# A hybrid encoder step: 28 pairs of input projections computed as seven block products, ahead of the attention

## The chip, the core and the metric

One core of one Trainium2 chip. The metric is the device time of one execution of the whole step in microseconds (us); lower is better. The engines are named as in the profile: PE multiplies matrices and writes PSUM, PEld is its loading of weights, DVE is the vector engine, ACT the engine of the activation functions, POOL the GpSimd engine, SP the queue from which nearly all DMAs are issued. Each engine takes its instructions in program order.

## The reference

A thousand and twenty-four new frames (the prompt) and 32 frames of a running stream (the sample) go through one layer. Both are 1024 channels wide, and the kernel treats them as 1056 columns. All inputs are float32.

```python
def mixer_inputs(x, norm_g, w_in, b_f, q_g, k_g):
    h = rmsnorm(x, norm_g)
    cols = lambda a, w: h @ w_in[:, a:a + w]
    q = rmsnorm(cols(OFF_Q, ATTN_WIDTH).reshape(B, T, N_HEADS, HEAD_DIM), q_g) * (HEAD_DIM ** -0.5)
    k = rmsnorm(cols(OFF_K, ATTN_WIDTH).reshape(B, T, N_HEADS, HEAD_DIM), k_g)
    v = cols(OFF_V, ATTN_WIDTH).reshape(B, T, N_HEADS, HEAD_DIM)
    logf = jax.nn.log_sigmoid((cols(OFF_F, N_HEADS) + b_f).astype(jnp.float32))
    ga = cols(OFF_GA, ATTN_WIDTH)
    u = cols(OFF_UA, CONV_WIDTH) * jax.nn.sigmoid(cols(OFF_UB, CONV_WIDTH))
    gb = cols(OFF_GB, CONV_WIDTH)
    ma, mb = cols(OFF_MA, D_MODEL), cols(OFF_MB, D_MODEL)
...
    ya = (o_attn.reshape(B, T, ATTN_WIDTH) * jax.nn.silu(ga)) @ w_pa
    yb = (jax.nn.silu(layernorm(conv, ln_g, ln_b)) * jax.nn.silu(gb)) @ w_pb
    m = jax.nn.sigmoid(ma) * ya + jax.nn.sigmoid(mb) * yb
    return x + m @ w_out
```

`o_attn` is causal softmax attention of 16 heads of 64 channels with a bias `C[t] - C[s]` from the running sum of `logf`; the sample attends over 512 cached frames and itself. `conv` is a causal depthwise convolution of `u` over 31 frames.

## The kernel before

**Tiles.** A tile of a projection is 128 output channels by all 1056 columns. Its weights are 8 blocks (kt) of 128x128, one for each 128 input channels. There are eight tiles each of `ua`, `ub`, `ga`, `ma`, `k`, `q`, `gb`, `mb` (the input projections; `v` and `f` are done in another form, 260 weight columns at a time, in line 582), and of `pb`, `pa` and `out` (the output projections).

**Three products for one.** Every float32 operand is split into a high and a low part in a reduced format (`xh`, `xl`; `wh`, `wl`). ACT makes `wh` by a cast of the loaded tile `raw` (line 91), POOL makes `wl = raw - wh` in three pieces 384, 384 and 256 wide (line 94). `mms` (line 102) then adds `wh*xh`, `wl*xh` and `wh*xl` in PSUM. A tile is 3 chunks of 352 columns, by 8 kt, by 3 products: 72 matmuls.

**Stages.** (1) The input is normalised, transposed and split, and the first `ua`, `ub` are computed. (2) `v` and `f`, with two more `u` tiles. (3) `k` and `q` tiles, `u` tiles 4 to 7 between them, and the eight `ga` tiles. (4) The attention, in blocks of 128 queries of one head: scores in `psS` (lines 917, 918), a mask and a maximum on DVE (920, 922), the exponential on ACT (925), a scaling on POOL (928), transposes on PE (945) into `pth` (ACT, 949) and `ptl` (DVE, 950), and the products with `V` (961, 962). Between the steps of a block, `fill(4)` puts four kt-steps of a further input projection (`gb`, `ma`, 22 tiles in all, evacuated at line 761) on PE. (5) Two last gate tiles, then `pa`, `pb` and `out`.

**The convolution.** For each of the 8 channel tiles, tap 0 is on ACT (line 255) and the other 30 taps are each one DVE instruction over 1086 columns that reads `u` and `y` from SBUF (line 258): 240 in all. Then `y` is kept in DRAM, and its sum and the sum of its squares are added to `mean` and `rstd` (lines 228, 235 on DVE, 236 on ACT, 241 on POOL). The layernorm's statistics are finished inside the attention; the normalisation, the SiLU and the gate (lines 1100 to 1109) run during the `pa` stage.

**What sets the order.** In stages 1 to 3 PE, DVE and ACT keep the order in which the program is written. Each kt-step of a projection calls `beat()`, which advances a tick. Work for the other engines is recorded by `later(n, fn)`, n ticks on, or taken from the list `taps` at `pace["rate"]` items per tick. A tick is three matmuls long. In the attention PE alone has a fixed order; a scheduler orders the rest. So an engine that falls behind has no way round: what is recorded behind a tap waits for it.

## Time and profile before

| what | value |
|---|---|
| median of three runs | 1407.84 us (1406.81 to 1408.3) |
| profiled execution: span, first to last instruction | 1405.2 us |
| PE busy in the span | 1393.8 us |
| DVE busy | 936.7 us |
| ACT busy | 637.7 us |
| POOL busy | 624.3 us |
| mean granted PE clock | 0.998 |

The page gives the profiled execution by its span alone; the median of the runs is 2.6 us above it. PE's matmuls are pipelined: a record lasts about twice as long as the spacing of two starts, so durations of PE are read from rows that count many matmuls over a stretch. Records of DVE, ACT and POOL are the instructions' own. Windows of the trace are given in us from the span's start; the attention lies between about 599 and 1100.

### The profile page before, as it was taken

The numbers are of one execution on the slowest core, as the hardware profiler recorded it, in microseconds if no ns is written. First come the engines' busy times: TensorE is split into PE (matmuls) and PEld (weight loads), VectorE is DVE, ScalarE is ACT, GpSimd is POOL, SyncE is SP. The second block draws the span as 40 slices with busy tenths as digits, with TensorE's granted clock in tenths as the row PEclk, the third lists the DMA queues.
The fourth block names the chain that finished last, engine by engine and source line by source line (L and its number), as shares of the span: only waits on it lengthen the run. The fifth ranks groups of instructions, "written<-read, shape, count | busy, mean of one in ns | idle before, by whom it ended". The sixth has DMA issues, their size and how long they took to land.

```text
span 1405.2 us, 24570 instructions
## 1 busy us (share of the span) xinstructions
PE 1393.8 (99%) x9255; PEld 1363.2 (97%) x9255; DVE 936.7 (67%) x1407; ACT 637.7 (45%) x1308; POOL 624.3 (44%) x665
## 2 busy tenths in 40 slices
PE   9999999999999999999999999999999999999999
PEld 8999999999999999999999999999999999999998
DVE  6688787888898999567677767755565487133111
ACT  6332334645464642255545656654554456232100
POOL 2324254557585875344333434333432267255320
PEclk9999999999999999999999999999999999999999
DMA  4253443424342483343546546453542688444431
GB/s 181 92 178 114 153 134 101 159 84 136 110 146 95 143 200 120 129 123 103 147 123 175 160 138 175 115 164 110 171 132 82 231 286 285 146 138 142 150 108 47
DMA packets 110614, 201.23 MB, mean 143 GB/s; under 512 B 17376, under 2 KB 74592, under 8 KB 110496
## 3 DMA queue, kind: packets, MB, share of 16 engines
q1 hardware_dynamic: 110352, 199.60, 45.4%
q8 instruction: 73, 1.20, 0.4%
q14 instruction: 45, 0.37, 0.1%
q10 hardware_dynamic: 144, 0.07, 0.0%
HBM read 129.78 MB, written 69.84 MB: 142 GB/s over the span
## 4 chain that ended last, share of the span: by engine, by line
PE 93%; DVE 3%; issue 2%; ACT 2%; POOL 1%; ACTq 0%; DVEq 0%; POOLq 0%
PE pj L102 68%; PE pjv L582 7%; PE ptr L945 4%; PE po L961 3%; PE po L962 3%; PE psS L917 2%; PE psS L918 2%; DVE nm L922 1%; PE po L895 1%; PE warm L345 1%; PE pst L706 1%; PE pst L705 1%; POOL wl L94 0%; PE ptx L427 0%; DVE y L258 0%
## 5 line engine op out<-in xcount | busy, mean ns | idle before, releaser
L102 PE MATMUL pj<-xh,wh 128*128 128x352 f32 (+2 forms) x1536 | 510.0, 332 | 3.8 <-ACT t L761 3.5
L102 PE MATMUL pj<-xl,wh 128*128 128x352 f32 (+2 forms) x1536 | 495.3, 322 | 0.2
L102 PE MATMUL pj<-xh,wl 128*128 128x352 f32 (+2 forms) x1536 | 494.0, 322 | 0.2 <-POOL wl L94 0.2
L94 POOL TENSOR_TENSOR wl<-raw,wh 128x384 fp32r<-128x384 f32 (+1 forms) x258 | 319.3, 1266 | 227.7 <-ACT wh L91 208.3
L258 DVE SCALAR_TENSOR_TENSOR y<-u,vec_t,y 128x1086 f32<-128x1086 f32 x240 | 379.6, 1582 | 11.6 <-ACT y L255 8.3
L102 PEld LDWEIGHTS pj<-xh,wh 128*128 128x128 f32 x1536 | 289.3, 188 | 11.8 <-ACT t L761 8.2
L102 PEld LDWEIGHTS pj<-xh,wl 128*128 128x128 f32 x1536 | 289.8, 189 | 0.8 <-POOL wl L94 0.5
L102 PEld LDWEIGHTS pj<-xl,wh 128*128 128x128 f32 x1536 | 289.2, 188 | 1.4 <-DVE xl L430 1.2
L928 POOL TENSOR_SCALAR P<-P,nm 128x128 f32<-128x128 f32 (+7 forms) x128 | 97.8, 764 | 223.7 <-DVE nm L927 190.2
L91 ACT CAST wh<-raw 128x1024 fp32r<-128x1024 f32 x86 | 90.1, 1048 | 111.3 <-PE pj L102 80.0
L925 ACT ACTIVATE P<-psS,nm 128x128 f32<-128x128 f32 (+7 forms) x128 | 95.7, 748 | 66.7 <-DVE nm L922 61.4
L949 ACT CAST pth<-ptr 128x512 fp32r<-128x512 f32 (+1 forms) x192 | 86.1, 484 | 74.3 <-PE ptr L945 73.3
L950 DVE TENSOR_TENSOR ptl<-ptr,pth 128x512 fp32r<-128x512 f32 (+1 forms) x192 | 100.7, 549 | 13.8 <-ACT pth L949 12.4
L922 DVE TENSOR_REDUCE nm<-psS 128x1 f32<-128x128 f32 (+7 forms) x128 | 96.5, 754 | 5.7
L723 POOL TENSOR_TENSOR ql<-qn,qh 128x352 fp32r<-128x352 f32 (+1 forms) x48 | 65.7, 1370 | 69.3 <-ACT qh L722 55.5
L945 PE MATMUL ptr<-ident,P 128*128 128x128 f32 x576 | 85.0, 274 | 0.0
L961 PE MATMUL po<-pth,V 128*128 128x256 f32 x320 | 79.2, 283 | 0.0
L962 PE MATMUL po<-ptl,V 128*128 128x256 f32 x320 | 78.6, 281 | 0.0
L945 PEld LDWEIGHTS ptr<-ident,P 128*128 128x128 f32 x576 | 69.8, 141 | 5.2
L920 DVE TENSOR_TENSOR psS<-psS,cmask 128x128 f32<-128x128 f32 x128 | 37.7, 294 | 54.3 <-PE psS L918 53.0
L582 PE MATMUL pjv<-vwh,xh 128*128 128x260 f32 x256 | 72.5, 283 | 0.0
L582 PE MATMUL pjv<-vwl,xh 128*128 128x260 f32 x256 | 72.4, 283 | 0.0
(205 smaller groups left out, 2518.5 us busy)
## 6 DMA issues: line engine op xcount, KB each, us to landing
raw<-wf SPq DMA_DIRECT2D x88, 512.0 KB
s_v<-vb SPq DMA_DIRECT2D x32, 256.0 KB
QB<-s_q SPq DMA_DIRECT2D x32, 256.0 KB
KB<-s_k SPq DMA_DIRECT2D x32, 256.0 KB
V<-s_v SPq DMA_DIRECT2D x16, 512.0 KB
kT<-qn SPq DMA_DIRECT2D x8, 528.0 KB
s_ga<-t SPq DMA_DIRECT2D x24, 176.0 KB
s_gb<-t SPq DMA_DIRECT2D x24, 176.0 KB
```

The source lines that it names most:

```text
L91: nc.scalar.copy(wh, raw)
L94: nc.gpsimd.tensor_sub(wl[:, k0:k1, :], raw[:, k0:k1, :], f32(wh[:, k0:k1, :]))
L102: nc.tensor.matmul(ps, a[:, kt, :], b(kt, sl), start=(first and n == 0), stop=(last and n == N - 1))
L258: t = nc.vector.scalar_tensor_tensor(y, u[:, i:i + CW], w, y, op0=ALU.mult, op1=ALU.add)
L582: nc.tensor.matmul(ps[:, :VC], a, b, start=(n == 0), stop=(n == 23))
L922: nc.vector.tensor_reduce(nm[:, 0:1], ps[:, :nb, :w], axis=AX.XY, op=ALU.max, negate=True)
L925: nc.scalar.activation(P[:, :nk].rearrange("p (b w) -> p b w", b=nb), ps[:, :nb, :w], AF.Exp, bias=nm[:, 0:1], accum_out=nm[:, 1:2])
L928: nc.gpsimd.tensor_scalar(P[:, :nk], P[:, :nk], nm[:, 2:3], 1.0, op0=ALU.mult, op1=ALU.mult)
L945: nc.tensor.transpose(pt[:, 128 * j:128 * j + 128], P[:, 128 * (4 * u + j):128 * (4 * u + j) + 128], ident)
L950: nc.vector.tensor_sub(ptl[:, js, qo], p3, f32(pth[:, js, qo]))
L961: nc.tensor.matmul(po[:, :256], V[:, j, :], pth[:, j, :], start=(j == 0), stop=False)
L962: nc.tensor.matmul(po[:, :256], V[:, j, :], ptl[:, j, :], start=False, stop=(j == njb - 1))
```

## The change

**Pairs.** 56 of the 64 tiles of input projections (all but `ua`, `ub` 0 to 3) are computed two at a time by Strassen's scheme in Winograd's form. The two weight tiles and the 1056 columns are cut into 2x2 blocks: weights of 128 outputs by 512 inputs, inputs of 512 by 528 columns. Seven block products of 24 matmuls, 264 columns wide, stand for the eight that two tiles amount to (line 889). For each pair DVE makes four sums of weight blocks (line 655, 128x512), ACT and POOL split seven blocks instead of two tiles (line 663), and DVE combines the products with five instructions (lines 864 to 876, 528 wide, PSUM and SBUF in). The sums of input blocks are made once, ahead of the first pair (lines 607 to 613, with POOL's part at 599). A pair is 56 ticks.

**Order.** All input projections, the whole convolution, the layernorm and the product of its result with the gate `gb` (lines 1092 to 1100, through DRAM) now stand before the attention. In the attention PE's filler is `pb` (seven tiles inside, one behind), one step at a time and from the 29th block on. Scores run five blocks ahead of the transposes (`LA`), not three. Behind the attention come `pa` and `out` alone.

```diff
-R_U, R_V, R_QK, R_G, R_A = 0.25, 0.17, 0.19, 0.27, 0.12
+R_U, R_V, R_T, R_S = 0.3, 0.25, 0.26, 0.15
+HB = 264
+HT = 2 * HB
+LA = 5
...
+    def t_build(j):
+        b11, b12, b22 = [tm.tile([128, HT], F32, name=a, tag=a) for a in ("b11", "b12", "b22")]
+        t1 = t1f[:, j, :]
+
+        def joined(b, k, s):
+            nc.gpsimd.tensor_add(b, f32(xh[:, k, s]), f32(xl[:, k, s]))
+
+        joined(b12, j, HI)
+        joined(b22, 4 + j, HI)
+
+        def lows():
+            joined(b11, 4 + j, LO)
+            nc.vector.tensor_sub(t3[1][:, j, :], b12, f32(t3[0][:, j, :]))
+
+        return [lambda: nc.vector.tensor_add(b11, f32(xh[:, j, LO]), f32(xl[:, j, LO])),
+                lambda: nc.vector.tensor_sub(t1, b11, b12),
+                lambda: (nc.vector.tensor_sub(b12, b12, b22), nc.scalar.copy(t3[0][:, j, :], b12)),
+                lambda: (nc.vector.tensor_add(b22, b22, t1), nc.scalar.copy(t2[0][:, j, :], b22)),
+                lows,
+                lambda: nc.vector.tensor_sub(t2[1][:, j, :], b22, f32(t2[0][:, j, :])),
+                lambda: (nc.vector.tensor_sub(b11, b11, b22), parts(t4, j, b11))]
...
+    pairs = [("gb", 0, "gb", 1), ("gb", 2, "gb", 3)]
+    for i, e in enumerate((4, 5, 0, 6, 0, 7, 0, 0)):
+        m = "ma" if i < 4 else "mb"
+        pairs += [("k", i, "q", i), (m, 2 * i % 8, m, 2 * i % 8 + 1)]
+        if e:
+            pairs += [("ub", e, "ua", e)]
+        if i == 5:
+            pairs += [("gb", 4, "gb", 5)]
+    pairs += [("gb", 6, "gb", 7)] + [("ga", f, "ga", f + 1) for f in range(0, 8, 2)]
+    NP = len(pairs)
+    BP = 56
...
+    def w_sum(i, dst, x, y, own=None):
+        w = W[i]
+        if own:
+            w[dst] = pw.tile([128, 4, 128], F32, name=own, tag=own)
+        else:
+            w[dst] = w[y]
+        nc.vector.tensor_add(w[dst], w[x], w[y])
+
+    def w_split(i, k):
+        raw = W[i][PROD[k][0]]
+        with tc.high_priority(offset=2000):
+            wh = pw.tile([128, 4, 128], F32R, name="swh", tag="swh", bufs=4)
+            nc.scalar.copy(wh, raw)
+            wl = pw.tile([128, 4, 128], F32R, name="swl", tag="swl", bufs=4)
+            nc.gpsimd.tensor_sub(wl, raw, f32(wh))
+        W[i][k] = wh, wl
+
+    def prepare(i):
+        if i >= NP:
+            return
+        s = S0[0] + i * BP
+        at(s - 30, lambda: w_sum(i, "s1", "a21", "a22", "s1"))
+        at(s - 27, lambda: w_sum(i, "s2", "s1", "a11", "s2"))
+        at(s - 24, lambda: w_sum(i, "s3", "a11", "a21"))
+        at(s + 23, lambda: w_sum(i, "s4", "s2", "a12"))
+        for k in range(7):
+            at(s + 8 * k - LEAD, lambda k=k: w_split(i, k))
+
...
+    PROD = (("a11", "b11", 0, True, True), ("s2", "t2", 1, True, True), ("s3", "t3", 2, True, True),
+            ("s1", "t1", 3, True, True), ("a12", "b21", 0, False, True), ("a22", "t4", 2, False, True),
+            ("s4", "b22", 3, False, True))
...
+            def low():
+                nc.vector.tensor_sub(s[0], s[2], f32(s[1]))
...
+            def scaled():
+                nc.vector.scalar_tensor_tensor(qn[:, sl], qn[:, sl], gv, s[2], op0=ALU.mult, op1=ALU.mult)
+
+            def out():
+                nc.scalar.copy(s[1][:, :n], qn[:, o:o + n])
+                nc.gpsimd.tensor_sub(s[0][:, :n], qn[:, o:o + n], f32(s[1][:, :n]))
+                nc.sync.dma_start(dst[0, f * 128:(f + 1) * 128, o:o + n], f32(s[1][:, :n]))
+                nc.sync.dma_start(dst[1, f * 128:(f + 1) * 128, o:o + n], f32(s[0][:, :n]))
...
+    def products(i):
+        s = S0[0] + i * BP
+        assert pace["tick"] == s
+        prepare(i + 1)
+        at(s + 34, lambda: raws_of(i + 2))
+        p = KIND.get(pairs[i][0], Gates)(s, *pairs[i])
+        ps = {}
...
+        def n2_out():
+            kept["n"] = ev.tile([128, HT], F32, name="n", tag="n")
+            nc.vector.tensor_sub(two(kept["n"]), ps[1], two(kept["v"]))
...
+        for t, fn in ((9, p1_out), (18, n2_out), (26, v3_out), (34, lambda: p.block(1, 1, c22)),
+                      (42, lambda: p.c11(ps[0])), (50, lambda: p.block(1, 0, c21)), (58, lambda: p.block(0, 1, c12))):
+            at(s + t, fn)
...
+        for k, (wn, xn, b, first, last) in enumerate(PROD):
+            wh, wl = W[i].pop(k)
+            oh, ol = OPS[xn]
+            if first:
+                ps[b] = bank("ABCD"[b])[:, :, :HB]
+            for c in range(2):
+                for kt in range(4):
+                    for n, (a, x) in enumerate(((wh, oh), (wl, oh), (wh, ol))):
+                        nc.tensor.matmul(ps[b][:, c, :], a[:, kt, :], x(kt, c), start=(first and kt == 0 and n == 0),
+                                         stop=(kt == 3 and n == 2), skip_group_check=not first)
+                    beat()
...
+    def c_tile(f, t):
+        b = {}
+
+        def load():
+            b["y"], b["g"] = y, g = [cps[0].tile([128, TT], F32, name=a, tag=a) for a in ("y3", "g3")]
+            nc.sync.dma_start(y, s_y[f])
+            nc.sync.dma_start(g, s_g["gb"][f])
+
+        def norm():
+            nc.vector.tensor_sub(b["y"], b["y"], mean)
+            nc.vector.tensor_mul(b["y"], b["y"], rstd)
+
+        def silu():
+            nc.scalar.activation(b["y"], b["y"], AF.Silu, bias=vcol(V_LNB, f), scale=vcol(V_LNG, f))
+
+        def out():
+            nc.vector.tensor_mul(b["y"], b["y"], b["g"])
+            nc.sync.dma_start(s_y[f], b["y"])
+
+        for d, fn in ((0, load), (34, norm), (40, silu), (45, out)):
+            at(t + d, fn)
...
+    def c_half(f):
+        c = ap.tile([128, TT], F32, name="c3", tag="c3")
+        nc.sync.dma_start(c, s_y[f])
+        nc.scalar.copy(c_h[:, f, :], c)
+        nc.gpsimd.tensor_sub(c_l[:, f, :], c, f32(c_h[:, f, :]))
...
+        def ev(c, sl, ps):
+            nc.vector.scalar_tensor_tensor(ts[c], ts[c], 1.0, ps, op0=ALU.add, op1=ALU.mult)
+            nc.sync.dma_start(s_ya[f, :, sl], ts[c])
+
+        return steps(("pb", f), lambda kt, sl: c_h[:, kt, sl], lambda kt, sl: c_l[:, kt, sl], pq, ev)
...
+    left = [8 * 24]
...
+    def fill(n, whole=False):
         for _ in range(n):
-            next(flow, None)
+            left[0] -= 1
+            if next(flow, None) and not whole:
+                break
...
+    for b in seq[:LA]:
+        start(b)
     for n, b in enumerate(seq):
...
+        if n + LA < len(seq):
+            start(seq[n + LA])
+        if n + LA + 2 < len(seq) and getattr(seq[n + LA + 2], "i", 1) == 0:
+            seq[n + LA + 2].head.load()
+        if n + LA + 3 < len(seq) and isinstance(seq[n + LA + 3], Sample):
+            seq[n + LA + 3].load()
+        if n % 3 == 1 and n < 25:
+            c_half(n // 3)
+        if n >= 28:
+            fill(1)
+        b.turn()
+        if n >= 28 and n % 2:
...
+    while left[0] > 24:
+        fill(1)
...
+    fill(24, True)
...
     def mk_pa(f):
-        sma = [sg2.tile([128, CH], F32, name="sma", tag="sma") for _ in range(3)]
-        for c in range(3):
-            nc.sync.dma_start(sma[c], s_g["ma"][f, :, csl(c)])
-            nc.scalar.activation(sma[c], sma[c], AF.Tanh, scale=0.5)
+        sma, yb = big("sma"), big("yb")
+        nc.sync.dma_start(sma, s_g["ma"][f])
+        nc.scalar.activation(sma, sma, AF.Tanh, scale=0.5)
+        nc.sync.dma_start(yb, s_ya[f])
...
-            nc.sync.dma_start(s_ya[f, :, sl], sma[c])
+            nc.vector.scalar_tensor_tensor(sma[:, sl], sma[:, sl], 1.0, ps, op0=ALU.add, op1=ALU.mult)
+            nc.vector.scalar_tensor_tensor(sma[:, sl], yb[:, sl], 1.0, sma[:, sl], op0=ALU.mult, op1=ALU.add)
+            nc.scalar.copy(mh[:, f, sl], sma[:, sl])
+            nc.gpsimd.tensor_sub(ml[:, f, sl], sma[:, sl], f32(mh[:, f, sl]))
```

**The order on the engines.** On DVE, ahead of the change, among the `k` and `q` tiles (`sql` is the low part of the squares, `qn` the scaled result, `y` a tap):

```order
L698 TENSOR_TENSOR sql_4154<-sqf_4152,sqh_4153 128x352
L258 SCALAR_TENSOR_TENSOR y_3194<-u_2273,vec_t_109,y_3194 128x1086
L698 TENSOR_TENSOR sql_4188<-sqf_4186,sqh_4187 128x352
L258 SCALAR_TENSOR_TENSOR y_4199<-u_3032,vec_t_109,y_4199 128x1086
L712 SCALAR_TENSOR_TENSOR qn_4116<-pj_4117,vec_t_109,ri_4207 128x352
L258 SCALAR_TENSOR_TENSOR y_4199<-u_3032,vec_t_109,y_4199 128x1086
L698 TENSOR_TENSOR sql_4230<-sqf_4228,sqh_4229 128x352
L258 SCALAR_TENSOR_TENSOR y_4199<-u_3032,vec_t_109,y_4199 128x1086
L712 SCALAR_TENSOR_TENSOR qn_4116<-pj_4157,vec_t_109,ri_4248 128x352
L698 TENSOR_TENSOR sql_4284<-sqf_4282,sqh_4283 128x352
```

And with the change, in the `k`, `q` pair and the gate pair behind it (`n`, `v`, `t` are the combinations of products, `rawa`, `rawb` and `s` weight sums, `sa` what `sql` was):

```order
L864 TENSOR_TENSOR n_4249<-psB_4194,v_4199 128x528
L819 TENSOR_TENSOR sa_4232<-sf_4234,sb_4233 128x528
L655 TENSOR_TENSOR rawa_3816<-s2_4033,rawa_3816 128x512
L254 SCALAR_TENSOR_TENSOR y_3662<-u_2322,vec_t_106,y_3662 128x1086
L655 TENSOR_TENSOR s1_4283<-rawb_4058 128x512
L867 TENSOR_TENSOR v_4199<-psC_4238,n_4249 128x528
L655 TENSOR_TENSOR s2_4308<-s1_4283,rawa_4056 128x512
L819 TENSOR_TENSOR sa_4286<-sf_4288,sb_4287 128x528
L254 SCALAR_TENSOR_TENSOR y_3662<-u_2322,vec_t_106,y_3662 128x1086
L655 TENSOR_TENSOR rawb_4058<-rawa_4056,rawb_4058 128x512
L832 SCALAR_TENSOR_TENSOR qn_4098<-qn_4098,vec_t_106,sf_4302 128x528
L870 TENSOR_TENSOR t_4337<-v_4199,psD_4272 128x528
```

Between two taps there now stand weight sums and combinations beside the work for keys and queries, and the scaling reads `qn` from SBUF where it read `pj` from PSUM.

On POOL, at the same two places, ahead of the change (`wl` is the low part of a weight tile, `ql` that of a key or query chunk):

```order
L723 TENSOR_TENSOR ql_3916<-qn_3741,qh_3915 128x352
L94 TENSOR_TENSOR wl_3929<-raw_3925,wh_3927 128x384 x2
L94 TENSOR_TENSOR wl_3929<-raw_3925,wh_3927 128x256
L723 TENSOR_TENSOR ql_3965<-qn_3741,qh_3964 128x352
L729 TENSOR_SCALAR qs_t_194<-qn_3741 128x32
L723 TENSOR_TENSOR ql_4000<-qn_3741,qh_3999 128x320
L94 TENSOR_TENSOR wl_4045<-raw_4041,wh_4043 128x384 x2
L94 TENSOR_TENSOR wl_4045<-raw_4041,wh_4043 128x256
```

and with it (`swl` is the low part of a weight block):

```order
L842 TENSOR_SCALAR qs_t_191<-qn_4854 128x32
L663 TENSOR_TENSOR swl_5001<-rawa_4601,swh_4999 128x512
L836 TENSOR_TENSOR sa_4863<-qn_4854,sb_4864 128x496
L663 TENSOR_TENSOR swl_5041<-rawb_4603,swh_5039 128x512
L663 TENSOR_TENSOR swl_5075<-rawa_4601,swh_5073 128x512
L663 TENSOR_TENSOR swl_5125<-rawa_4850,swh_5123 128x512
L836 TENSOR_TENSOR sa_4977<-qn_4892,sb_4978 128x528
L663 TENSOR_TENSOR swl_5174<-s2_5102,swh_5172 128x512
L836 TENSOR_TENSOR sa_5026<-qn_4854,sb_5027 128x528
L663 TENSOR_TENSOR swl_5220<-rawb_4852,swh_5218 128x512
```

Seven blocks of 512 columns now stand for each two tiles, in the order in which PE needs them, and the subtractions for keys and queries stand between them.

On PE, where the attention begins, ahead of the change (`pj` is the filler, and twelve of its matmuls stand between two blocks):

```order
L917 MATMUL psS<-KB,QB 128x384
L918 MATMUL psS<-KA,QA 128x384
L917 MATMUL psS<-KB,QB 128x512
L918 MATMUL psS<-KA,QA 128x512
L945 MATMUL ptr_6626<-ident,P 128x128
L102 MATMUL pj<-xh,wh 128x352
L102 MATMUL pj<-xh,wl 128x352
L102 MATMUL pj<-xl,wh 128x352
```

and with the change:

```order
L1248 MATMUL psS<-KB,QB 128x384
L1249 MATMUL psS<-KA,QA 128x384
L1276 MATMUL ptr_10098<-ident,P 128x128
L1248 MATMUL psS<-KB,QB 128x448
L1249 MATMUL psS<-KA,QA 128x448
...
L1276 MATMUL ptr_10130<-ident,P 128x128 x2
L1248 MATMUL psS<-KB,QB 128x512
L1249 MATMUL psS<-KA,QA 128x512
...
L1276 MATMUL ptr_10151<-ident,P 128x128 x3
```

No filler stands between the first blocks; it comes in with the 29th.

More of the change, by code (lines that the diff above doesn't have):

```diff
@@ L562, in build @@
         if c == 2:
-            pace["rate"] = R_U
-            u_proj(2, pj)
-            while ("y", 0) not in sides or len(taps) > 62:
+            while ("done", 0) not in sides:
                 pump(1)
@@ L1056, in build @@
             b.values()
-    for _ in flow:
-        pass
+    while left[0] > 24:
+        fill(1)
     p2.close()
```

576 lines of the change are left out of this document (316 added, 260 removed).

## The prediction

> **What bounds the kernel now.** I first read the page's busy time by engine and its chain of waits.
>
> ```profile
> span 1405.2 us, 24570 instructions
> PE 1393.8 (99%) x9255; PEld 1363.2 (97%) x9255; DVE 936.7 (67%) x1407; ACT 637.7 (45%) x1308; POOL 624.3 (44%) x665
> PE 93%; DVE 3%; issue 2%; ACT 2%; POOL 1%; ACTq 0%; DVEq 0%; POOLq 0%
> PE pj L102 68%; PE pjv L582 7%; PE ptr L945 4%; PE po L961 3%; PE po L962 3%; PE psS L917 2%; PE psS L918 2%; DVE nm L922 1%; PE po L895 1%; PE warm L345 1%; PE pst L706 1%; PE pst L705 1%; POOL wl L94 0%; PE ptx L427 0%; DVE y L258 0%
> ```
>
> PE bounds all stages: 93% of the chain is PE, 68% the projections' matmuls. Averages over stages hide a near second, so next I read windows (PE, PEld, DVE, ACT, POOL, then clock, DMA share, GB/s).
>
> ```profile
> 400.00:575.00 175.00, 175.00 (x1101) 174.97 (x1100) 162.05 (x131) 77.28 (x137) 116.58 (x75) 1.00 0.45 138
> 475.00:500.00 25.00, 25.00 (x159) 25.00 (x158) 24.89 (x24) 15.00 (x30) 22.03 (x16) 1.00 0.42 141
> 600.00:1100.00 500.00, 496.08 (x3447) 475.69 (x3446) 334.29 (x765) 270.68 (x636) 183.39 (x320) 0.99 0.47 135
> ```
>
> Among the keys, queries and gates (400 to 575) DVE works 162.05 of 175 us, and from 475 to 500 it works 24.89 of 25 us while PE still never stops. DVE stands just behind PE there. In the attention it works 334.29 of 500. The clock is full throughout, so it is no term. The same window by groups, with two rows of quiet moments, shows what fills DVE:
>
> ```profile
> L258 DVE SCALAR_TENSOR_TENSOR y<-u,vec_t,y 128x1086 f32<-128x1086 f32 x80 | 134.5, 1682 | 4.1 <-ACT y L255 2.5
> L698 DVE TENSOR_TENSOR sql<-sqf,sqh 128x352 fp32r<-128x352 f32 x16 | 14.5, 909 | 3.7 <-ACT sqh L695 3.7
> L712 DVE SCALAR_TENSOR_TENSOR qn<-pj,vec_t,ri 128x352 f32<-128x352 f32 x9 | 5.2, 573 | 0.1
> L712 DVE SCALAR_TENSOR_TENSOR qn<-pj,qg,ri 128x352 f32<-128x352 f32 x9 | 5.0, 561 | 2.2 <-ACT ri L709 2.2
> ...
> L94 POOL TENSOR_TENSOR wl<-raw,wh 128x384 fp32r<-128x384 f32 x30 | 49.5, 1669 | 27.2 <-ACT wh L91 27.2
> L94 POOL TENSOR_TENSOR wl<-raw,wh 128x256 fp32r<-128x256 f32 x15 | 25.0, 1665 | 0.0
> L723 POOL TENSOR_TENSOR ql<-qn,qh 128x352 fp32r<-128x352 f32 x12 | 21.0, 1752 | 19.6 <-ACT qh L722 12.7 <-DMA s_k<-ql 6.3 <-DMA s_q<-ql 0.6
> L723 POOL TENSOR_TENSOR ql<-qn,qh 128x320 fp32r<-128x320 f32 x7 | 9.5, 1352 | 0.0
> ```
>
> ```profile
> 52.88 9.67 DVE L258 SCALAR_TENSOR_TENSOR y<-u,vec_t,y 128x1086 f32<-128x1086 f32 x7 [0.98 <-ACT y L255]
> 489.21 0.52 DVE L698 TENSOR_TENSOR sql<-sqf,sqh 128x352 fp32r<-128x352 f32 x1
> 588.27 2.68 POOL L94 TENSOR_TENSOR wl<-raw,wh 128x384 fp32r<-128x384 f32 x3
> 494.13 5.83 POOL L94 TENSOR_TENSOR wl<-raw,wh 128x384 fp32r<-128x384 f32 x3
> 495.77 7.30 DVE L258 SCALAR_TENSOR_TENSOR y<-u,vec_t,y 128x1086 f32<-128x1086 f32 x4
> ```
>
> Seven taps in a row with POOL still take 9.67 us, 1.38 each; in the window the mean is 1.68. A `sql` takes 0.52 quiet, 0.91 in the window. POOL's three pieces of one weight tile take 2.68 us with DVE idle and 5.83 us at 494, while the taps of DVE beside them take 7.30/4 = 1.83. So DVE and POOL instructions that both read two operands from SBUF hold each other up. The `qn` scaling, which reads `pj` from PSUM, keeps to 0.57.
>
> **The change part by part.**
>
> *PE.* The window's matmul price and that of a narrower one come from long unbroken pieces of the chain of waits:
>
> ```profile
> 344.93 26.78 PE pj L102 x168
> 160.19 32.63 PE pjv L582 x270
> ```
>
> 352 columns: 26.78/168 = 159.4 ns; 260 columns: 32.63/270 = 120.9 ns. The slope is 38.5/92 = 0.42 ns a column, so 264 columns come to 122.5 ns. A pair took 144 x 159.4 = 22.95 us and takes 168 x 122.5 = 20.58: 2.37 saved, for 28 pairs **-66.4 us**. This holds if PE is fed.
>
> *DVE's own work.* Besides the rows above I use
>
> ```profile
> 1128.73 1.34 DVE L1092 TENSOR_TENSOR al<-a,ah 128x1056 fp32r<-128x1056 f32 x1 [1.34 <-ACT ah L1091]
> 1092.61 1.16 DVE L950 TENSOR_TENSOR ptl<-ptr,pth 128x512 fp32r<-128x512 f32 x2
> ```
>
> 1.34 for 1056 columns from SBUF gives 0.66 for 528 and 0.65 for 512; 512 with one operand in PSUM take 1.16/2 = 0.58, my price of a combination. A `k`, `q` pair and the gate pair behind it (I call the two a duo; there are eight) have, counted in the order, about 16 taps (22.1), 8 weight sums (5.2), 4 lows of squares and 4 scalings from SBUF (5.3), 10 combinations (5.8) and half a column sum (1.3): 39.7 us. PE needs 2 x 20.58 and 2.0 for the 16 small matmuls of the norms: 43.1. That leaves 8%, where 400 to 575 had, without collisions, (175 - 162.05 + 30.4)/175 = 25%; the 30.4 follows.
>
> *Collisions.* The window's price: taps 80 x 0.30 = 24.2, lows 16 x 0.39 = 6.2, together 30.4 us over 64 subtractions of POOL (30, 15, 12 and 7, mean width 341): 0.475 each, by width 0.71 for 512. The few wide sums on POOL in that window are left out, which makes the price high by a tenth perhaps. A duo has 14 `swl` and 4 subtractions for keys and queries: 18 x 0.71 = 12.8. DVE then needs 52.5 against 43.1: +9.4, for eight duos +75. An `ub` pair (four of them) has 7 taps (9.7), 4 weight sums (2.6), 5 combinations (2.9) and the product with the gate in four pieces (2.6), 17.8, and 7 x 0.71 = 5.0: 22.8 against 20.58, +9 in all. The other gate pairs have no keys and no such product (15.2 + 5.0 = 20.2) and hold. A combination is recorded some 14 ticks (5 us) before its PSUM bank is written again, so DVE may lag by that, -5: 75 + 9 - 5 = **+79 us**. Behind the late instruction on DVE stand the combinations, which free the banks, and the weight sums, from which ACT and POOL make the next products' weights; PE waits for both. Bounds: 0 if POOL's reads cost nothing (39.7 is under 43.1); at the top each of POOL's instructions adds its whole quiet time, 1.34 for 512 (half of 2.68): 39.7 + 18 x 1.34 = 63.8, eight times 20.7 too much, and 4 x 6.6 for the `ub` pairs, together 192. I take the measured price, since it comes from the same two engines in the same kind of work.
>
> The Trainium skill (SBUF — State Buffer, Who interferes with whom) calls the shared read path an exclusive lock: a DVE instruction with two SBUF inputs and a GpSimd instruction that reads SBUF block each other for the whole instruction, and a DVE instruction with at most one SBUF input is free of it. By that the sum would have +192 in place of +79. The trace agrees on who is hit (taps and `sql` yes, `qn` from PSUM no), but the wait it shows is 0.475 us of the some 0.89 that 341 columns take quiet.
>
> *Sums of input blocks.* Ahead of the first pair DVE gets 36 instructions of 528 (24), 6 taps (8.3) and about 7 of other work, 39 us in 96 ticks of three matmuls, 45.9 us of PE; POOL's 12 joins (0.73) and the pieces of four weight tiles (0.475) add some 14. That is 7 too much. ACT stood at 77.28 of 175 us and the DMAs at a share of 0.45 in the window; both go on with the same kinds of work, ACT's casts in halves. The normalisation's three passes for eight tiles (24 x 1.34 = 32 us) stand in the last five pairs, where no tap is left: 32 + 5 x 5.5 in 103 us, hidden, and so are its 24 DMAs in SP's queue, unless head 0's first load stands behind the last gates' stores; then the attention's first blocks wait. At the attention's end 12 steps, one `pb` tile and most of a `pa` tile (27 us) cover the splitting of its output. For these seams I take **+8**, bounds 0 and 25.
>
> *Attention.*
>
> ```profile
> L258 DVE SCALAR_TENSOR_TENSOR y<-u,vec_t,y 128x1086 f32<-128x1086 f32 x30 | 42.0, 1400 | 0.0
> ```
>
> Twenty-two filler tiles of 72 x 159.4 ns = 11.48 us are 252.5 of the 500 us; without them PE has 247.5/132 = 1.88 us a block. DVE, without its 30 taps, has (334.29 - 42.0)/132 = 2.21. From the 29th block on the filler (1.5 steps of 0.48) brings PE to 2.6, above DVE. The first 28 blocks have none. There a block takes at least about DVE's 2.21, and at most 500/132 = 3.79, the pace at which the chain of maximum, exponential, scaling and transposes was hidden before with scores three blocks ahead; I take the middle, 3.0, since nothing in the trace shows bare blocks: 28 x (3.0 - 1.88) = **+31**, bounds 9 and 53. The eight reloads of the gated tiles, their ACT casts and POOL subtractions (8 x 2.7 = 22 us of 84) run beside it.
>
> *Sum:* 1405.2 - 66.4 + 79 + 31 + 8 = 1456.8. The median of the runs (1407.84) lies 2.6 above the profiled span: **1459 us**.
>
> **The rivals.**
>
> *A, faster: PE keeps its pace.* If POOL's instructions slip into DVE's combinations and idle gaps, a duo fits into 43.1 as long as one of them costs under (43.1 - 39.7)/18 = 0.19 us; the input sums then cost less too. 1405.2 - 66.4 + 31 + 5 + 2.6 = 1377. For it: POOL stood idle for 58 of 175 us in the window above, so there is room, and from 475 to 500 PE didn't wait for a DVE without a gap. Against it: 0.19 is a quarter of the measured price, and the order gives POOL no choice of its moment.
>
> *D, half the price.* With fewer DVE instructions open to collision (10 of some 44 in a duo read PSUM), 0.355 for 512 columns: a duo needs 46.1, 3.0 x 8 = +24, the `ub` pairs nothing. 1405.2 - 66.4 + 24 + 31 + 8 + 2.6 = 1404, a little faster than before. Against it: in the window too 18 scalings of `qn` and the products for `u` read PSUM, and the price is an average over them as well.
>
> *B, the attention starves instead.* DVE keeps up, but every block takes 2.7 us, not 1.88, and the filler, put at fixed places, fills none of it: 132 x 0.82 = 108. 1405.2 - 66.4 + 108 + 8 + 2.6 = 1457. It decides as soon as one block's chain of five engines is longer than the 5 blocks (10 us) by which the scores run ahead. Against it: three blocks ahead, with 3.79 each, hid it before.
>
> *E, full blocking,* the +192 above: 1405.2 - 66.4 + 192 - 5 + 31 + 8 + 2.6 = 1567. Against it stands the window's mean.
>
> **How the numbers follow.** My forecast (DVE sets the pace of the pairs) 0.50, A 0.27, D 0.15, B 0.05, E 0.03. Differences within 0.2% (3 us) can't be told from none; D alone spreads over them, by a fifth of its share and a little more of its neighbours': 0.05. Faster is A and most of the rest of D, 0.36; slower 0.59. The likeliest case's own range is 1410 to 1500: a collision of 0.55 and bare blocks of 2.2 give 1409, 0.85 and 3.6 give 1500. For 8 in 10 the range reaches down into A: 1370 to 1500.
>
> **What would show it.** Right: in the pairs' stage DVE busy in nearly all of the time and PE waiting for `n`, `v`, `t` and weights; taps at 1.7 us or more; the 28 pairs in about 670 us, not 592 (28 x 20.58 and the norms' 16); the attention in about 355 us (247.5 + 6.5 x 11.48 + 31). The matmul term is wrong if unbroken 264-column pieces aren't near 122.5 ns. The DVE term is wrong if taps are near 1.5 and PE is without gaps there. The attention term is wrong if its first 28 blocks take much less, or more, than 84 us.

## The result and the profile after

The changed kernel takes 1584.39 us (median of four runs, 1584.12 to 1590.64) against 1407.32 before: a ratio of 1.1275, 95% interval 1.1253 to 1.1297. It is slower, as forecast, but by 177 us and not by 51, and lies outside the stated range of 1370 to 1500. The profiled execution is the slowest of the four, 6 us above the other three, and the attention takes 397 to 405 us in the ten runs below that keep the seven products and the gates' tanh, whatever else they change: differences of that size are not told from none.

The head of the page and the shares of the chain by engine:

```profile
span 1588.8 us, 26535 instructions
PE 1403.5 (88%) x9963; PEld 1345.9 (85%) x9963; DVE 1214.8 (76%) x1638; ACT 687.7 (43%) x1341; POOL 775.0 (49%) x690
PE 20%; DMA 10%; DVE 5%; ACT 2%; issue 1%; SPq 1%; POOL 0%; ACTq 0%; DVEq 0%; POOLq 0%
```

PE is no longer busy throughout: 88% of a longer span. The chain can be followed back only to 957 us here, and before the last stage it runs through DMAs, DVE and ACT. The same program divided by its stages, before and then after (PE, PEld, DVE, ACT, POOL, clock, DMA share, GB/s):

```profile
225.00:601.00 376.00, 375.41 (x2355) 374.28 (x2354) 317.37 (x295) 183.13 (x333) 235.03 (x173) 1.00 0.42 131
601.00:1100.00 499.00, 495.08 (x3441) 474.69 (x3440) 334.29 (x765) 270.68 (x636) 183.39 (x320) 0.99 0.48 136
1100.00:1405.00 305.00, 301.75 (x1873) 301.46 (x1871) 112.36 (x139) 94.79 (x122) 125.59 (x107) 1.00 0.52 175
```

```profile
235.00:846.00 611.00, 528.23 (x4001) 518.26 (x4002) 589.18 (x507) 252.18 (x408) 399.06 (x225) 0.94 0.28 98
846.00:974.00 128.00, 113.17 (x857) 110.87 (x856) 86.80 (x87) 57.09 (x83) 59.61 (x38) 0.95 0.57 196
974.00:1380.00 406.00, 344.09 (x2317) 311.56 (x2316) 287.97 (x719) 240.82 (x569) 157.32 (x288) 0.92 0.58 156
1380.00:1588.00 208.00, 202.40 (x1261) 200.96 (x1259) 56.95 (x96) 45.05 (x58) 68.06 (x72) 1.00 0.45 150
```

| stage | before | after | tiles moved, at 11.48 us | net |
|---|---|---|---|---|
| up to the stage | 225 | 235 | | +10 |
| ahead of the attention (after: 23 and 5 pairs) | 376 | 739 | +24 tiles, +275.5 | +88 |
| attention | 499 | 406 | -15.5 tiles, -178 | +85 |
| behind it | 305 | 208 | -8.5 tiles, -98 | +1 |

A tile's 11.48 us is the prediction's price, 72 matmuls of 159.4 ns. The loss has two halves: the pairs cost 88 us more than the plain tiles they stand for would have, and the attention gave back only 93 of the 178 us of filler that was taken out of it. In the first 23 pairs DVE is busy 589 of 611 us. Its groups there, and POOL's (from 240 to 860):

```profile
L254 DVE SCALAR_TENSOR_TENSOR y<-u,vec_t,y 128x1086 f32<-128x1086 f32 x175 | 320.9, 1834 | 2.2 <-ACT y L251 0.7
L655 DVE TENSOR_TENSOR rawa<-s,rawa 128x512 f32<-128x512 f32 x24 | 31.6, 1315 | 1.4 <-POOL swl L663 1.4
...
L832 DVE SCALAR_TENSOR_TENSOR qn<-qn,qg,sf 128x528 f32<-128x528 f32 x16 | 21.7, 1354 | 0.6 <-ACT sf L829 0.6
...
L864 DVE TENSOR_TENSOR n<-psB,v 128x528 f32<-128x528 f32 x24 | 16.7, 697 | 2.4 <-PE psB L889 2.0 <-ACT v L860 0.4
```

```profile
L663 POOL TENSOR_TENSOR swl<-rawa,swh 128x512 fp32r<-128x512 f32 x70 | 122.1, 1750 | 106.9 <-ACT swh L661 75.7 <-issue 30.5 <-POOL u L273 0.7
```

Taps take 1.83 us (1.38 quiet), weight sums up to 1.32 (0.65 estimated from quiet rows), scalings 1.35; a combination, which reads PSUM, keeps to 0.70. What PE waits for in the 28 pairs (us in all, times, longest):

```profile
PE psB L825 <- ACT sf L828: 32.8, 8, 5.9
PE psD L889 <- DVE qn L870: 11.6, 5, 3.0
PE psC L889 <- DVE v L867: 11.2, 5, 4.8
```

The first of them leads to DVE as well: L825 needs a bank that ACT empties into `sf` (L828), and ACT stands there for a low part that DVE makes late.

```profile
ACT sf L828 <- DVE sa L819: 22.4, 8, 3.9
```

### The profile page after: what moved, and what is told of

The parts are those of the page before. It is cut to its first block, busy times and chain, and to the rows that moved or that the text cites. A ratio compares the mean times of both kernels' runs of the same rounds, so it can differ in the third digit from the quotient of the medians.

```text
span 1588.8 us, 26535 instructions
## 1 busy us (share of the span) xinstructions
PE 1403.5 (88%) x9963; PEld 1345.9 (85%) x9963; DVE 1214.8 (76%) x1638; ACT 687.7 (43%) x1341; POOL 775.0 (49%) x690
## 5 line engine op out<-in xcount | busy, mean ns | idle before, releaser
L663 POOL TENSOR_TENSOR swl<-rawa,swh 128x512 fp32r<-128x512 f32 x84 | 143.5, 1714 | 130.1 <-ACT swh L661 94.6
L95 POOL TENSOR_TENSOR wl<-raw,wh 128x384 fp32r<-128x384 f32 (+1 forms) x90 | 88.3, 1008 | 142.2 <-ACT wh L92 126.9
L889 PE MATMUL psD<-xh,swh 128*128 128x264 f32 x448 | 132.4, 296 | 22.8 <-DVE qn L870 11.6
L889 PE MATMUL psA<-xh,swh 128*128 128x264 f32 x448 | 132.7, 296 | 10.5 <-DVE u L295 9.5
L663 POOL TENSOR_TENSOR swl<-s,swh 128x512 fp32r<-128x512 f32 x56 | 95.1, 1698 | 88.0 <-ACT swh L661 79.5
L889 PE MATMUL psA<-xh,swl 128*128 128x264 f32 x448 | 132.9, 297 | 4.3 <-POOL swl L663 4.2
L889 PE MATMUL psD<-xh,swl 128*128 128x264 f32 x448 | 131.1, 293 | 2.2 <-POOL swl L663 2.2
L889 PE MATMUL psA<-xl,swh 128*128 128x264 f32 x448 | 132.0, 295 | 0.0
L889 PE MATMUL psD<-xl,swh 128*128 128x264 f32 x448 | 130.8, 292 | 0.0
L663 POOL TENSOR_TENSOR swl<-rawb,swh 128x512 fp32r<-128x512 f32 x56 | 113.9, 2034 | 17.9 <-ACT swh L661 17.7
```

The costliest lines, as they stand in the source:

```text
L95: nc.gpsimd.tensor_sub(wl[:, k0:k1, :], raw[:, k0:k1, :], f32(wh[:, k0:k1, :]))
L663: nc.gpsimd.tensor_sub(wl, raw, f32(wh))
L889: nc.tensor.matmul(ps[b][:, c, :], a[:, kt, :], x(kt, c), start=(first and kt == 0 and n == 0), stop=(kt == 3 and n == 2), skip_group_chec ...
```

## The experiments

All but the last are one profiled run each, beside one run of the kernel before on the same chip (1405 to 1408 us). Lengths of stages go from the first matmul of one to the first or last matmul of the next.

**e1: DVE without its taps, and e2: POOL without its subtractions.** In the first, a condition on line 254; in the second, lines 662 to 664:

```diff
+            if i == KC - 1:
-            nc.vector.scalar_tensor_tensor(y, u[:, i:i + CW], w, y, op0=ALU.mult, op1=ALU.add)
+                nc.vector.scalar_tensor_tensor(y, u[:, i:i + CW], w, y, op0=ALU.mult, op1=ALU.add)
```

> Leaves out 29 of the 30 DVE taps of each channel tile (232 of 240), nothing else. Theory (DVE's throughput sets the pace of the pairs): DVE falls far below PE's need, PE runs at 20.6 us a pair, the 28 pairs take 595 to 625 us in place of 740, the granted clock there is back near 1.0 and the span is 1430 to 1475 us. Rival (the chain of weight sums, casts, splits and PSUM banks makes PE wait, however idle DVE is): the pairs stay above 680 us and the span above 1530.

```diff
-            nc.gpsimd.tensor_sub(wl, raw, f32(wh))
-        W[i][k] = wh, wl
+        W[i][k] = wh, wh
```

> Leaves out POOL's 196 subtractions for the low parts of the weight blocks (PE reads the high part a second time, so its work is the same). Theory (their reads of SBUF slow DVE): a pair of pairs with keys goes from 55.2 to 45 or 46 us, taps from 1.83 to 1.45 or 1.5 us, the 28 pairs to 620 to 660 us, the span to 1465 to 1510. Rival (DVE's own work and its fixed order alone make the excess): the pairs stay above 700 us, the span above 1545.

Measured: 1451.69 and 1456.28 us. The pairs take 614 and 609 us, in place of 740. The windows of the first 23 pairs, of e1 and then e2, and e2's taps and weight sums (from 240 to 720):

```profile
223.00:714.00 491.00, 488.37 (x4001) 487.64 (x4001) 286.62 (x339) 259.79 (x411) 304.13 (x226) 1.00 0.36 123
```

```profile
233.00:723.00 490.00, 488.86 (x4001) 488.19 (x4002) 457.14 (x507) 256.01 (x407) 94.22 (x64) 1.00 0.35 121
```

```profile
L254 DVE SCALAR_TENSOR_TENSOR y<-u,vec_t,y 128x1086 f32<-128x1086 f32 x172 | 250.2, 1454 | 4.2 <-ACT y L251 2.8
L655 DVE TENSOR_TENSOR rawa<-s,rawa 128x512 f32<-128x512 f32 x23 | 15.7, 684 | 0.0
```

The rivals fall. e1 lies in its theory's range; e2 gained more than its theory said (609 us for 620 to 660). PE runs the 23 pairs in 490 us, its own price, with the clock at 1.00, whether DVE loses its taps or POOL its subtractions. So DVE's load decides, and 161 subtractions on POOL cost DVE 589.2 - 457.1 = 132 us, 0.82 each. And neither run reaches the old time: the attention takes 404 and 403 us in them too.

**e5: the subtractions on DVE.**

```diff
-            nc.gpsimd.tensor_sub(wl, raw, f32(wh))
+            nc.vector.tensor_sub(wl, raw, f32(wh))
```

> The 196 subtractions for the low parts of the weight blocks are done by DVE, not by POOL; nothing is left out. Theory (what POOL takes off DVE in this stage it gives back as collisions): a pair with keys and the gate pair behind it cost DVE 39.7 + 14 x 0.65 + 4 x 0.71 = 51.6 us, less than the 55.2 measured, so the pairs get no longer, 700 to 740 us, with taps near 1.45 us. Rival (POOL's help is worth its work): 9.1 more for each of the eight and 4.6 for each other pair, 28 pairs in 840 us or more, a span above 1680.

Measured: 1581.72 us, the pairs 734. In the first 23 DVE is busy 550 us with that work on top, less than the 589 it needed while POOL did it:

```profile
234.00:832.00 598.00, 526.43 (x4001) 516.13 (x4002) 549.74 (x666) 250.91 (x408) 82.01 (x64) 0.94 0.29 100
```

The forecast holds, the rival falls. POOL's help in this stage is worth less than nothing to DVE: 0.82 us a subtraction lost, 93/161 = 0.58 more when DVE does it itself (550 against e2's 457). But 39 us less of DVE's work made these 23 pairs only 13 us shorter, and PE still waits 103 us in the 28 pairs, as against 107. So the amount of DVE's work alone doesn't give the time; that the place of an instruction in DVE's fixed order counts too is likely, but no run varies it alone.

**e3, e6: eight plain products in the same order.** The products, from PROD of e6 (e3 has bank 0 in place of 2 for the last two, so each pair waits for the copy of the bank it wrote last):

```diff
+    PROD = (("a21", "b12", 0, True), ("a22", "b22", 0, False), ("a11", "b11", 2, True), ("a12", "b21", 2, False),
+            ("a21", "b11", 3, True), ("a22", "b21", 3, False), ("a11", "b12", 2, True), ("a12", "b22", 2, False))
```

> The same pairs in the same order by eight plain block products of 24 matmuls: no weight sums, no input sums, no combinations; four blocks are split, not seven; ACT copies the results from PSUM. Theory: DVE is relieved (28.7 us of its own for a pair with keys and the gate pair behind it, and 8.5 of collisions, against 49 of PE), so PE sets the pace with 192 x 122.5 ns = 23.5 us a pair: 28 pairs in about 675 us, less than the 740 of the seven products, and a span of about 1515. Rival (the order of work ahead of the attention makes PE wait, not the seven products): above 720 us for the pairs, a span above 1560.

> As the kernel of eight plain products, but the fourth result has the PSUM bank of the second, so that no pair waits for the copy of the bank written last. Theory: the pairs now run at PE's pace, 23.5 us each and 24.5 with the norms, 28 pairs in 675 to 695 us against 726 and against the 740 of the seven products; span 1495 to 1515. Rival (something else holds the pairs): above 715 us.

Measured: e3 1548.15 us, pairs 726, in its rival's range by a fault of my bank plan; e6, with that mended, 1500.57 us, pairs 680 as forecast. The window of e6's first 23 pairs:

```profile
222.00:778.00 556.00, 553.89 (x4558) 552.79 (x4558) 392.51 (x300) 241.92 (x382) 247.02 (x156) 1.00 0.33 111
```

With 14% more matmuls the pairs take 60 us less, and the whole kernel 84 less: the sums of input blocks go too, 13 us ahead of the pairs, and the attention is 388 us, 18 under that of the profiled execution. Here the seven products lose to eight.

**e7: the last five pairs without the normalisation.**

```diff
-    for f in range(8):
-        c_tile(f, lns + 108 + 18 * f)
```

> Leaves out the normalisation of the convolution's eight tiles in the last five pairs (loads, three DVE passes, SiLU, stores); the statistics stay. Theory (DVE's three passes in a row delay combinations behind them): the last five pairs, 128.5 us, come down to 105 to 115 and PE's waits on v and t there vanish; the attention's first blocks start sooner after the last pair, together 15 to 30 us off the span of 1588.8. Rival (the statistics' chain through PSUM bank B makes the waits): above 122 us.

Measured: 1568.80 us. The last five pairs take 115 us, at the edge of what was forecast, against 128 (PE's own price is 102 to 103); the attention's 398 in place of 406 is within the spread. Half of the last pairs' excess goes with the normalisation (its DVE passes, its SiLU and its DMAs together); what holds the rest is open, since no run leaves out the statistics.

**e10: the kernel before, with a thin filler.**

```diff
-NFILL = 22
-R_U, R_V, R_QK, R_G, R_A = 0.25, 0.17, 0.19, 0.27, 0.12
+NFILL = 6
+R_U, R_V, R_QK, R_G, R_A = 0.25, 0.17, 0.19, 0.27, 0.45
...
-            fill(4 if b.i > 2 or b.head.h != 8 else 0)
+            fill(1)
```

> The kernel before the change with one thing altered: 6 filler tiles in the attention, one step to a block, and 16 more gate tiles behind it (22 and 2 before; the taps in the attention go at a higher rate, so that all of them still stand there). No Strassen, no new order ahead of the attention. Theory (with a quarter of the filler the blocks can't keep PE busy, whatever stands ahead): the attention falls from 499 only to 390 to 410 us, not to 499 - 16 x 11.48 = 316, and the span rises to 1480 to 1500. Rival (the attention's excess is of the changed kernel's making: its gate loads, reloads and LA): 316 to 345 us and a span of 1405 to 1435.

Measured: 1471.33 us, 66 above the run of the kernel before. The attention takes 381 us where 247.5 + 6 x 11.48 = 316 would be PE's price:

```profile
600.00:981.00 381.00, 328.06 (x2291) 293.40 (x2290) 326.32 (x765) 235.70 (x572) 140.39 (x272) 0.98 0.49 132
```

The attention lies under the 390 to 410 of the theory and far above the 316 to 345 of the rival: no Strassen is needed to lose 65 us, only fewer matmuls between the blocks. This attention still holds 30 taps (42 us of DVE by the prediction's row), which the changed one doesn't, so its 65 us can't be carried over as they are.

**e4, e8: the attention without the filler's transfers, and without the reloads of the gated tiles.** e4:

```diff
-            nc.sync.dma_start(ts[c], s_g["mb"][f, :, csl(c)])
-            with tc.issue_after(sides["tables"].ins):
-                nc.scalar.activation(ts[c], ts[c], AF.Tanh, scale=0.5)
+            nc.gpsimd.memset(ts[c], 0.0)
...
+            if f == 7:
-            nc.sync.dma_start(s_ya[f, :, sl], ts[c])
+                nc.sync.dma_start(s_ya[f, :, sl], ts[c])
```

e8 in addition puts two memsets in the place of the load, cast and subtraction of `c_half`.

> Leaves out the loads of the mb gate for the seven pb tiles in the attention and the stores of their results (their factor is set to zero). Theory (in SP's queue the loads of the next head wait behind those loads and stores, which wait for buffers and for DVE): the attention goes from 406 us, first scores to last values, to 360 to 380, the span to 1545 to 1565. Rival (the chain of engines inside a block makes the waits): it stays above 395 us.

> Leaves out the loads and stores of the pb filler as before, and also the eight loads, casts and subtractions of the gated tiles in the attention's first 25 blocks. Theory (the DMAs fill the queue and the engines when the first heads load, the DMA share being 0.99 there): the first 100 us of the attention, PE busy 75 of 100 us, come to 80 to 88, the attention of 374 us to about 355, which is the bare blocks' own price. Rival (without filler the chain of engines in a block is bare whatever the DMAs do): it stays at 370 or more.

Measured: e4 1559.88 us, the attention 374, as forecast by the theory; but its reason, SP's queue, is tested below and falls. e8 1554.03 us, the attention 367, between the 355 of its theory and the 370 of its rival. Its first 100 us hold 77 us of PE, against 75 in e4; the first filler matmul comes 82 us behind the attention's start, not 90. So the reloads cost some of the first blocks' time, and most of their gaps stay without them.

**e9, e12, e13, e14, e16, e17: which part of the transfers costs these 32 us?** By the medians it is 25 (1584.39 to 1559.88), since the profile compared with is the slowest of its four. e9 gives the gates more buffers, e12 another queue, e13 loads them a tile ahead, e16 ties the tanh to the filler tile before, e14 leaves out the stores, e17 the tanh. The lines that differ, of e9, e12, e13 and e16:

```diff
+        far = (None, mean, rstd)[f % 3]
+        ts = [sg.tile([128, CH], F32, name="smb", tag="smb", bufs=4) if far is None else far[:, csl(c)] for c in range(3)]
...
+            nc.gpsimd.dma_start(ts[c], s_g["mb"][f, :, csl(c)])
+            nc.gpsimd.dma_start(s_ya[f, :, sl], ts[c])
...
+        if f < 7:
+            ahead(f + 1)
...
+            with tc.issue_after((sides["evac"] if f else sides["tables"]).ins):
```

and of e14 and e17:

```diff
+            if f == 7:
+                nc.sync.dma_start(s_ya[f, :, sl], ts[c])
...
-            with tc.issue_after(sides["tables"].ins):
-                nc.scalar.activation(ts[c], ts[c], AF.Tanh, scale=0.5)
```

> The changed kernel with nothing left out; the gate tiles of the pb filler have three homes in turn (their own four buffers, and the two tiles of the layernorm's statistics, which are free by then), so that a load needn't wait for a store. Theory (ACT and SP stand in line behind loads that wait for a buffer): most of the 32 us that came off the attention without those transfers come off here too, 376 to 386 us in place of 406, span 1558 to 1570. Rival (the transfers themselves, or the stores' wait for DVE in SP's queue, make the wait): above 398 us.

> The changed kernel with nothing left out; the pb filler's gate loads and its stores are issued from POOL's queue, not from SP's. Theory (in SP's queue the stores wait for DVE, 95 us in all, and the next head's loads stand behind them): the attention comes from 406 to 375 to 390 us, the span to 1560 to 1575. Rival (ACT, in its fixed order, waits for the gate's transfer wherever it is issued, or the transfers only take DMA time): above 398 us, span above 1580.

> The changed kernel with nothing left out; the gates of the pb filler are loaded one whole filler tile ahead (about 16 blocks), into three homes in turn, from SP's queue; their tanh stays at the start of the tile. Theory (ACT keeps a fixed order and stands 30 us behind loads that are issued too late, and the exponentials stand behind it): ACT's waits on those loads vanish and the attention comes from 406 to 370 to 388 us, span 1555 to 1573. Rival (the stores, which wait for DVE in SP's queue ahead of the next head's loads, or the transfers themselves): 396 us or more.

> Leaves out the stores of seven pb tiles' results, while their gates are loaded as before. By the theory of ACT's wait for the loads the attention stays at 395 us or more; by the rival (the stores in SP's queue) it comes to 370 to 388.

> As the kernel that loads the gates a tile ahead, but their tanh may only be placed behind the last evacuation of the filler tile before. (In the trace of that kernel a load still stood 2.4 us ahead of its tanh: both had been placed as soon as the buffer was free.) Theory (ACT, in its fixed order, stands behind transfers that take longer than its order was made for): ACT's waits on these loads vanish and the attention comes to 370 to 390 us. Rival (the price without the transfers, 374, comes from something else that left with them, ACT's tanh among it): 395 us or more.

> Leaves out the tanh of the pb filler's gates in the attention, and nothing else: loads and stores stay, and DVE, which uses the gates 8 filler steps later, is the one that needs them. Theory (ACT stands behind those transfers, 30 us of waits): with nothing on ACT that waits for them the attention comes to 370 to 385 us. Rival (the transfers cost by what they do in SP's queue or in the DMAs): 393 us or more; the 21 tanh are 10 us of ACT's own work.

Measured, the attention: e9 405 us, e12 399, e13 399, e14 400, e16 404, e17 373 (spans 1590.5, 1585.2, 1583.9, 1583.0, 1590.5, 1556.9). The window of e17:

```profile
975.00:1349.00 374.00, 335.43 (x2318) 306.59 (x2318) 286.69 (x718) 230.78 (x546) 157.39 (x288) 0.94 0.62 167
```

The gains forecast for e9, e12, e13 and e16 didn't come (405 to 399 is the spread); that e14 would bring none and e17 the whole was forecast. One run more, e11, has e6's products and e9's buffers: 1506.61 us and an attention of 394, against 1500.57 and 388 of e6, where 15 to 25 us less were forecast; there too the buffers gained nothing. In the changed kernel ACT waits for the gates' loads, and PE for exponentials behind them (waits in the attention of ACT and of PE, and one of the waits):

```profile
ACT smb L1145 <- DMA smb<-s_mb: 29.8, 13, 4.2
```

```profile
PE psS L1248 <- ACT P L1256: 22.6, 13, 6.0
```

```profile
1109.17 0.50 ACT L1145 ACTIVATE smb<-smb 128x352 f32<-128x352 f32 x1 [4.18 <-DMA smb<-s_mb]
```

Buffers and queues don't help, because the scheduler puts the tanh right behind its load: in e13 the load of a `smb` chunk is issued at 1088.9 and its tanh at 1091.3, and in e16, which was to part them, at 1091.7 and 1094.0. ACT's waits for these loads stay at 24 to 30 us in e9, e12, e13, e14 and e16. With the tanh alone gone, loads and stores all there, the whole gain of e4 is there (373 for 374 us; 26 us by the medians). That shows ACT's place in it; that it is the wait and not the 21 tanh themselves (10 us of an ACT that is busy 241 of 406) is argued, not shown.

**e15: scores three blocks ahead.**

```diff
-LA = 5
+LA = 3
```

> The changed kernel with scores three blocks ahead of the transposes, as before the change, not five. If the chain of engines in a block is what leaves PE idle and five blocks cover more of it, the attention grows by 10 us or more; if the two PSUM tiles for scores bound how far PE may run ahead, it changes by less than 6 us either way.

Measured: 1583.92 us, the attention 397. That is 9 us under the profiled execution, but its time is that of the other three of the changed kernel (1584.12 to 1584.57): no difference is shown. Five blocks ahead cover nothing that three don't; the forecast of a growth missed.

**e18: both causes mended.** e6, and the tanh where the gates are written, ahead of the attention:

```diff
-            self.fn = AF.Silu if g[0] == "g" else None
+            self.fn = AF.Silu if g[0] == "g" else AF.Tanh if g == "mb" else None
+            self.sc = 0.5 if g == "mb" else 1.0
```

> Nothing is left out: eight plain products with the better banks, and the tanh of the mb gates made when the gates are written, ahead of the attention, not in it. Theory (the two causes add up, and the thin filler stays): pairs 675 to 690 us, the attention of 388 us down to 360 to 372, the median 1472 to 1486, ratio to the kernel before 1.046 to 1.057. Rival (something else of the changed order costs less than the thin filler is blamed for): below 1440.

Measured: 1495.31 us (median of four), a ratio to the kernel before of 1.0636, interval 1.0618 to 1.0653; 9 us above the range expected. The attention is 365 us as forecast, 23 under e6's, but the pairs went from 680 to 696: PE waits 15.0 us for banks that ACT empties late, now that it makes the tanh there. The pairs and the attention:

```profile
222.00:918.00 696.00, 679.76 (x5529) 676.76 (x5529) 435.51 (x338) 318.43 (x481) 272.64 (x178) 0.99 0.38 126
918.00:1283.00 365.00, 333.06 (x2313) 304.96 (x2314) 283.20 (x717) 229.93 (x544) 151.55 (x280) 0.95 0.60 159
```

No version tried here beats the kernel before. Of the 89 us left, about 43 are the attention with its thin filler (365 us for 322 of PE's work) and 45 the pairs (696 us, where the plain tiles of before come to 376 + 275.5).

## Why the prediction was wrong

**The sign and the mechanism on DVE were right.** DVE set the pace of the pairs, and collisions with POOL decided it (e1, e2, e5). The single terms: 264 columns at 122.5 ns, and a pair of 20.58 us, measured 20.4 where nothing holds PE (e1, e2). DVE's own work with the keys' collisions came to 434 + 23 = 457 us for the first 23 pairs by my prices; e2 shows 457.1. That this fits to a tenth is partly luck: in e2 a combination took 0.70 us, not my 0.58, and a scaling from SBUF 0.91, not 0.66. The price of a collision was 0.71 and measured 0.82, worth 18 us over 161.

**The pairs were still 69 us short** (671 forecast, 740 measured). In the first 23 pairs it was 43 (611 for 568): 18 from that price, 5 from the lag that I subtracted, and the rest because a DVE in a fixed order idles even when it is the bound (611 us for 589 of work). By pairs, 16 of the 43 are the other gate pairs, of which I said that they hold: numbers 0, 1 and 18 took 25 to 26 us. Another 25 came from the last five pairs, which I called "hidden": I compared sums of work there (60 us in 103), and e7, without the normalisation, gives half of it back; that its three passes in a row delay a combination that PE waits for is the likely way, not shown by itself.

**The attention was the other large miss: 406 us where 353 follow from my sum.** The failed step is the fill from the 29th block on, "brings PE to 2.6, above DVE", which I took for hidden, with nothing for the tanh of the filler's gates. The windows of the first 91 us and of the rest:

```profile
974.00:1065.00 91.00, 61.71 (x344) 51.93 (x343) 60.31 (x149) 57.88 (x128) 49.40 (x69) 0.79 0.76 206
1065.00:1380.00 315.00, 282.38 (x1974) 259.63 (x1974) 227.66 (x570) 182.94 (x442) 107.92 (x220) 0.96 0.53 141
```

The first filler matmul starts at 1071, so the first 28 blocks took 97 us for 84, and the other 104 took 309, or 2.97 each, not 2.6. Of these 39 us too much, 27 belong to the tanh behind a load, which I had not costed at all though it is a moved step with DMAs of its own: in e17 the same blocks take 282 us, 2.71 each (302 to 311 in the ten runs that keep the tanh). The other 12 stay with the thin filler. The 13 us of the first blocks are not their own price: in e3 and e6, with eight products, they take 81 and 80 us, and in e8, without the reloads that I had put "beside it", 82. So 3.0 us for a bare block stood, and what is over seems to come with the reloads and with work that the seven products leave at the end of the pairs; the runs don't part the two.

My upper bound of 53 for the attention was the pace of the old blocks over 28 blocks only; it covered neither the other 104 nor the tanh, and the range with it was too narrow. Rival B named a starving attention, and I gave it 0.05 as an alternative to the DVE bound; the two came together. Its size was wrong too: 108 us over PE's price, where 406 - 322 = 84 were measured, 27 of them the tanh's.

The pairs' 69 and the attention's 53 leave 10 of the 132 us between my sum of 1456.8 and the profiled span. Three are the seams, 10 + 1 in the table for 8. Seven are an error in the sum: by the windows of before, 56 plain tiles with the work among them stand for 376 + 275.5 = 651.5 us, and less 66.4 that is 585, where PE's own price for the pairs, 592 with the norms, is what e1 and e2 bear out in their first 23.

**Rival A was wrong by more than its condition.** Even with PE at its own pace in the first 23 pairs (e1, e2) the kernel stays at 1452 and 1456 us, not 1377, since the attention and the last pairs don't depend on it.

**E fell as forecast.** A subtraction of 512 columns adds 0.82 us to DVE, not its whole 1.34; that the time came out above E's 1567 is the attention's doing.

## What to carry to other kernels

Price work that fills another stage's gaps by what that stage does without it: taking 178 us of matmuls out of this attention shortened it by 93, and taking 184 out of the old kernel's by 118. A scheme that trades an eighth of the matmuls for vector work pays only where the vector engine has that time free *with* the collisions that POOL's instructions add; count both before counting matmuls. And an instruction that waits for a DMA on an engine with a fixed order can be paid for by everything behind it (here some 27 us for the gates' tanh), so put it where the data have long arrived, and look at the order on that engine to see that it is there.

## What the runs showed of the hardware

**Waits cost PE its clock.** The granted clock was 1.00 before; it fell to 0.94 in the pairs and 0.92 in the attention. A wait in the changed kernel, and matmuls in the third and fourth microsecond behind it:

```profile
383.83 0.53 PE L889 MATMUL psD<-xh,swh 128*128 128x264 f32 x1 [3.01 <-DVE qn L870]
384.16 0.42 PE L889 MATMUL psD<-xh,swl 128*128 128x264 f32 x1
384.38 0.42 PE L889 MATMUL psD<-xl,swh 128*128 128x264 f32 x1
...
387.39 0.28 PE L889 MATMUL psD<-xh,swh 128*128 128x264 f32 x1
387.51 0.28 PE L889 MATMUL psD<-xh,swl 128*128 128x264 f32 x1
```

Starts lie 0.22 us apart for 3.4 us, and then 0.12. By the starts of all 4704 matmuls of the pairs, 307 are 0.20 to 0.24 us apart: 30 us of the 740, beside 107 us in the waits themselves. A wait is counted here from start to start, less the 0.12 of a matmul, so the one shown is 3.16. In the first 23 pairs every wait of 3.15 us or more was followed by 10 to 26 such matmuls; of those from 0.7 to 2.6 us only two, of 1.95 and 1.98, were, and the others by two or three at most. In the last five pairs waits of 2.50 and 2.07 were followed by 13 and 14, and one of 3.14 by one only, so the length of a wait alone doesn't decide it. The Trainium skill (TensorE: Matmul & The Clock Gate, HAM oscillation — how this bites in real kernels) asks for no idle gap above about 3.4 us; the direction agrees, but here gaps of 3.2 us, and four times of 1.9 to 2.5 us, were enough.

**A collision's price is neither nothing nor the whole.** 0.82 us of DVE for each POOL subtraction of 512 columns that takes 1.34 quiet (half of the prediction's 2.68), with 34 of a duo's 44 DVE instructions open to it; combinations that read PSUM took 0.70 with POOL busy and without.
